# A residual-add RMSNorm whose second tile deals one of its rows unevenly to the DMA engines

## The chip, the cores and the metric

The kernel runs on one core of one Trainium2 chip. The metric is the device time of one execution in microseconds. Times of many executions are given as a median, and one execution was profiled.

## The reference

```python
def reference(x, residual, gamma, eps):     # x, residual: 32 x 2048 x 2048 float32
    z = x + residual
    rms = np.sqrt(np.mean(z ** 2, axis=-1, keepdims=True) + eps)
    return (z / rms * gamma).astype(np.float32)
```

Flattened, there are 65,536 rows of 2048 numbers (8 KB a row). Each row of x and of the residual is read once and each row of the output written once: 1610.6 MB in all.

## The kernel before

**Tiles.** The rows are cut into 74 tiles. A tile of k rows puts k consecutive rows of the input on each of the 128 partitions. The first two tiles (`lead`, line 42) have 3 and 5 rows a partition, the other 72 have `R` = 7. x is loaded into one of two buffers `z[0]`, `z[1]` (even and odd tiles), where everything is computed in place, and the output is stored from there. The residual is loaded into `r_area`, which has room for 11 rows. Even tiles use it from row 4, odd ones from row 0, so that two residuals overlap in the middle; `parts` (line 108 on) splits each tile in two such that the overlapping rows are added first.

**Engines.** Four programs run side by side and meet only at semaphores.

- SyncE issues every DMA (`sync_program`, line 249, and `sp_turn`, line 145). At the start: x and r of tile 0, four small loads of gamma, r and x of tile 1. Then, in the turn of tile i: wait until tile i-1 is scaled, store it (L149); wait until the first part of tile i is added, load r of tile i+1 (L140); wait until the store of tile i-1 has landed, load x of tile i+1 (L134). This order is written out by hand for all tiles; it is no loop on the engine.
- VectorE (`dve_turn`) adds r to x in two parts (L170), then for each part takes the reciprocal of the root (L195) and scales each row by it and by gamma (L175).
- ScalarE (`act_turn`, `act_part`) squares each row and sums it up (L221), then takes the root (L229).
- GpSimd only waits for a last signal (`fin`) from SyncE and clears the semaphores (L328 to L331).

The last tile is handled in four pieces (`tail`), so that its stores begin early.

**Loops.** VectorE and ScalarE run the first `LO` = 3 tiles written out, then a hardware loop over two tiles at a time up to tile `HI` (70 is the last in the loop), then tiles 71 and 72 written out, then the last tile, 73.

**Gamma.** It is loaded to four partitions of `stage`, which is a part of `r_area` that VectorE has set to zero (L274), and spread over all partitions by a shuffle (L276).

[...]

Of the kernel before, what the change touches and what calls it, by code (L numbers as in the profile page):

```python
# [9 lines left out]
def kernel(  # L10
# [14 lines left out]

    nc = tc.nc
    P = nc.NUM_PARTITIONS
    fp32 = mybir.dt.float32  # L30
# [3 lines left out]
    x_f = x.flatten_outer_dims()  # L34
    r_f = residual.flatten_outer_dims()
    o_f = out.flatten_outer_dims()

    n_rows, D = x_f.shape
    R = 7
    STEP = 4  # L40
    U = 16
    lead = [3, 5]
    n_full = (n_rows // P - sum(lead)) // R
    sizes = lead + [R] * n_full
    starts = [0]
    for k in sizes:
        starts.append(starts[-1] + P * k)
    assert starts[-1] == n_rows
    n_tiles = len(sizes)
    last = n_tiles - 1  # L50

    LO = 3
    n_iter = (last - 1 - LO) // 2
    HI = LO + 2 * n_iter
    assert n_iter >= 1

    def rows(t, i):
        k = sizes[i]
        return t[starts[i] : starts[i] + P * k, :].rearrange("(p r) m -> p r m", r=k)

    inv_d = 1.0 / float(D)

    def sb(name, shape):
        return ctx.enter_context(nc.sbuf_tensor(name, shape, fp32))
# [6 lines left out]
    def sem(name):  # L71
        sems.append(ctx.enter_context(nc.semaphore(name)))
        return sems[-1]
# [3 lines left out]
    z = [sb(f"z{p}", [P, R, D]) for p in range(2)]  # L77
    r_area = sb("r_area", [P, R + STEP, D])
    eps_tile = sb("eps_tile", [P, 1])
    ssq = [[sb(f"ssq{p}{h}", [P, 4]) for h in range(2)] for p in range(2)]  # L80
    rms = [[sb(f"rms{p}{h}", [P, 4]) for h in range(2)] for p in range(2)]
    rstd = [[sb(f"rstd{p}{h}", [P, 4]) for h in range(2)] for p in range(2)]
    tail_ssq = sb("tail_ssq", [P, R])
    tail_rms = sb("tail_rms", [P, R])
    tail_rstd = sb("tail_rstd", [P, R])
# [5 lines left out]
    ev = {k: [sem(f"{k}{p}") for p in range(2)] for k in names}  # L91
# [2 lines left out]
    dve = sem("dve_own")  # L94
    act = sem("act_own")
    s_tail = sem("s_tail")
    fin = sem("fin")
    tail_ev = {k: sem(f"tail_{k}") for k in ("add", "rms", "done")}


    tail = [(0, 2), (2, 4), (4, 6), (6, 7)]

    def entry(i):
        if i == 0:
            return R + STEP - sizes[0]
        return 0 if i % 2 else STEP

    def parts(i):
        if i == 0:
            return [(0, 2), (2, sizes[0])]  # L110
        k = sizes[i] if i < 2 else R
        return [(STEP, k), (0, STEP)] if i % 2 else [(0, R - STEP), (R - STEP, R)]

    class Turn:

# [12 lines left out]
    def inc(ins, kind, i):  # L128
        return ins.then_inc(ev[kind][i % 2], U)


    def load_x(sp, t, d=0):
        i = t.i + d
        inc(sp.dma_start(out=z[i % 2][:, : sizes[i], :], in_=rows(x_f, i)), "x_in", i)  # L134

    def load_r(sp, t, d=0):
        i = t.i + d
        e = entry(i)
        inc(
            sp.dma_start(out=r_area[:, e : e + sizes[i], :], in_=rows(r_f, i)),  # L140
            "r_in",
            i,
        )

    def sp_turn(sp, t):
        i = t.i
        t.wait(sp, "done", -1)
        inc(
            sp.dma_start(out=rows(o_f, i - 1), in_=z[(i - 1) % 2][:, : sizes[i - 1], :]),  # L149
            "s_out",  # L150
            i - 1,
        )
        if i == last:
            return
        t.wait(sp, "add_a")
        load_r(sp, t, 1)
        t.wait(sp, "s_out", -1)
        if i + 1 == last:
            for k, (a, b) in enumerate(tail):
                sp.dma_start(  # L160
                    out=z[last % 2][:, a:b, :], in_=rows(x_f, last)[:, a:b, :]
                ).then_inc(x_tail[k], U)
        else:
            load_x(sp, t, 1)


    def add(v, i, a, b):
        e = entry(i)
        s = z[i % 2][:, a:b, :]
        return v.tensor_add(out=s, in0=s, in1=r_area[:, e + a : e + b, :])  # L170

    def scale(v, i, a, b, rs, c=0):
        for g in range(a, b):
            s = z[i % 2][:, g, :]
            ins = v.scalar_tensor_tensor(  # L175
                out=s,
                in0=s,
                scalar=rs[:, c + g - a : c + g - a + 1],
                in1=gamma_tile[:, :],
                op0=mult,  # L180
                op1=mult,
            )
        return ins

    def dve_turn(v, t, own):
        i, p = t.i, t.p
        t.wait(v, "x_in")
        t.wait(v, "r_in")
        (a0, b0), (a1, b1) = parts(i)
        inc(add(v, i, a0, b0), "add_a", i)  # L190
        inc(add(v, i, a1, b1), "add_b", i)
        for h, (a, b) in enumerate(parts(i)):
            n = b - a
            t.wait(v, "rms_a" if h == 0 else "rms_b")
            v.reciprocal(out=rstd[p][h][:, :n], in_=rms[p][h][:, :n]).then_inc(dve, U)  # L195
            v.wait_ge(dve, own(i, h))
            ins = scale(v, i, a, b, rstd[p][h])
        inc(ins, "done", i)
# [34 lines left out]
    def act_turn(s, t, chain):  # L233
        i, p = t.i, t.p
        for h, (a, b) in enumerate(parts(i)):
            chain.wait()
            t.wait(s, "add_a" if h == 0 else "add_b")
            inc(
                act_part(s, chain, z[p], a, b, ssq[p][h], rms[p][h][:, : b - a]),
                "rms_a" if h == 0 else "rms_b",  # L240
                i,
            )

    stage = r_area[:, 5:7, :].rearrange("p r m -> p (r m)")
    stage = stage.rearrange("p (a b) -> p a b", a=16)[:, :, : D // 16]

    def sync_program(sp):
        load_x(sp, Turn(0))  # L250
        load_r(sp, Turn(0))

        sp.wait_ge(tail_ev["add"], 1)
        for q in range(4):
            sp.dma_start(  # L255
                out=stage[32 * q : 32 * q + 1],
                in_=gamma.partition_broadcast(1).rearrange("p (a b) -> p a b", a=16),
            ).then_inc(g_in, U)
        load_r(sp, Turn(1))
        load_x(sp, Turn(1))  # L260
        for i in range(1, n_tiles):
            sp_turn(sp, Turn(i))
        for k, (a, b) in enumerate(tail):
            sp.wait_ge(tail_ev["done"], k + 1)
            sp.dma_start(
                out=rows(o_f, last)[:, a:b, :], in_=z[last % 2][:, a:b, :]
            ).then_inc(s_tail, U)
        sp.wait_ge(s_tail, U * len(tail))
        sp.wait_ge(ev["s_out"][(last - 1) % 2], ((last - 1) // 2 + 1) * U)
        sp.sem_inc(fin, 1)  # L270

    def vector_program(v):
        v.memset(eps_tile[:, :], float(eps))  # L273
        v.memset(stage, 0.0).then_inc(tail_ev["add"], 1)  # L274
        v.wait_ge(g_in, 4 * U)
        v.stream_shuffle(gamma_tile[:, :].rearrange("p (a b) -> p a b", a=16), stage, [0] * 32)  # L276
        for i in range(LO):
            dve_turn(v, Turn(i), lambda i, h: (2 * i + h + 1) * U)
        with v.Fori(0, 2 * n_iter, 2) as it:
            for i in range(LO, LO + 2):  # L280
                dve_turn(v, Turn(i, it), lambda i, h: it * (2 * U) + (2 * i + h + 1) * U)
        for i in range(HI, last):
            dve_turn(v, Turn(i), lambda i, h: (2 * i + h + 1) * U)
        base = 2 * last * U
        t = Turn(last)
        t.wait(v, "r_in")

        def tail_scale(k):
            a, b = tail[k]
            v.wait_ge(tail_ev["rms"], k + 1)  # L290
            v.reciprocal(out=tail_rstd[:, a:b], in_=tail_rms[:, a:b]).then_inc(dve, U)  # L291
            v.wait_ge(dve, base + (k + 1) * U)
            scale(v, last, a, b, tail_rstd, a).then_inc(tail_ev["done"], 1)

        for k, (a, b) in enumerate(tail):
            v.wait_ge(x_tail[k], U)
            add(v, last, a, b).then_inc(tail_ev["add"], 1)
            if k:
                tail_scale(k - 1)
        tail_scale(len(tail) - 1)  # L300

    def scalar_program(s):
# [13 lines left out]
        for k, (a, b) in enumerate(tail):  # L316
# [3 lines left out]
                s, chain, z[last % 2], a, b, tail_ssq[:, a:b], tail_rms[:, a:b]  # L320
            ).then_inc(tail_ev["rms"], 1)

    sync_program(nc.sync)
    vector_program(nc.vector)
    scalar_program(nc.scalar)


    nc.gpsimd.wait_ge(fin, 1)  # L328
    ids = [a.num for a in sems]
    assert ids == list(range(ids[0], ids[0] + len(ids)))  # L330
    nc.gpsimd.sem_clear(range(ids[0], ids[-1] + 1))  # L331


# [33 lines left out]
```

## Time and profile before

| | us |
|---|---|
| Median of 10 executions | 3726.25 (3726.1 to 3726.57) |
| The profiled execution, its own time | 3726.18 |
| Its span in the profile | 3724.4 |
| VectorE busy | 2302.4 (62%) |
| ScalarE busy | 1072.4 (29%) |
| GpSimd busy | 0.2 |
| Data queue, share of 16 engines | 99.9% |
| Moved | 1610.69 MB, 432 GB/s over the span |

The page divides the span into 40 equal slices. For each it gives the busy share of an engine in tenths, the mean busy share of the 16 DMA engines in the same way, and the GB/s that they moved. Lines such as L170 are lines of the kernel's file. A DMA's instruction is short (0.3 to 0.6 us for SyncE to issue one); the transfer itself takes until it lands. For the 7-row tiles the median from issue to landing is 27.2 us for r, 33.8 for x and 34.4 for a store. A window gives the same numbers for any stretch of the span; the DMA share there is the mean over 16 engines, so one engine alone gives 0.06.

### The profile page before, as it was taken

Reading aid. Unit: us, or ns where it says so; the run is one execution under the profiler, and the core shown is the slowest. Engines: PE = TensorE matmul, PEld = TensorE weight load, DVE = VectorE, ACT = ScalarE, POOL = GpSimd, SP = SyncE. Lnnn points to the kernel's source line nnn. Section 1 sums busy time; section 2 is a strip of 40 time slices with the busy share of each in tenths; the row PEclk is TensorE's granted clock in tenths of the full one; section 3 lists DMA queues with packets and bytes.
Section 4 is the critical chain, followed back from the end, with each engine's and each line's share of the span. In section 5 each row is a group of like instructions: output and inputs, shape, how many; then the busy total and the mean of one; then the engine's idle time right before and its main releaser. Section 6 shows DMA issues by size and latency. Waiting matters only on the chain.

```text
span 3724.4 us, 3652 instructions
## 1 busy us (share of the span) xinstructions
DVE 2302.4 (62%) x816; ACT 1072.4 (29%) x1176; POOL 0.2 (0%) x4
## 2 busy tenths in 40 slices
DVE  5666665566665566665566665566665566655566
ACT  2233322233322233322233322233322233322233
POOL 0000000000000000000000000000000000000000
DMA  9999999999999999999999999999999999999999
GB/s 421 431 434 434 435 434 434 434 434 435 434 434 434 434 434 434 434 434 434 434 433 434 434 434 434 434 434 434 434 434 434 434 434 434 434 434 434 433 435 398
DMA packets 32964, 1610.69 MB, mean 432 GB/s; under 512 B 3712, under 2 KB 3776, under 8 KB 3776
## 3 DMA queue, kind: packets, MB, share of 16 engines
q1 hardware_dynamic: 32960, 1610.66, 99.9%
q14 instruction: 4, 0.03, 0.0%
HBM read 1073.77 MB, written 536.87 MB: 432 GB/s over the span
## 4 chain that ended last, share of the span: by engine, by line
DMA 66%; DVE 22%; issue 9%; ACT 2%; SPq 0%; DVEq 0%; ACTq 0%
DMA out_dram<-z 33%; DMA z<-in_x_dram 33%; DVE z L170 15%; DVE z L175 7%; ACT sq_junk L221 1%; DMA r_area<-in_gamma_dram 0%; ACT rms L229 0%; DVE rstd L195 0%; DVEq L126 0%; SPq L255 0%; DVE r_area L274 0%; ACTq L209 0%; ACTq L126 0%; DVE tail_rstd L291 0%; SPq L160 0%
## 5 line engine op out<-in xcount | busy, mean ns | idle before, releaser
L170 DVE TENSOR_TENSOR z<-z,r_area 128x8192 f32<-128x8192 f32 (+2 forms) x150 | 1109.4, 7436 | 1253.3 <-DMA z<-in_x_dram 1227.5
L221 ACT ACTIVATE sq_junk<-z 128x2048 f32<-128x2048 f32 x512 | 963.4, 1882 | 2617.8 <-DVE z L170 2606.4
L175 DVE SCALAR_TENSOR_TENSOR z<-z,rstd,gamma_tile 128x2048 f32<-128x2048 f32 x505 | 1153.5, 2343 | 5.2
L195 DVE RECIPROCAL rstd<-rms 128x4 f32<-128x4 f32 (+2 forms) x146 | 25.2, 173 | 130.9 <-ACT rms L229 130.9
L221 ACT ACTIVATION_READ_ACCUMULATOR sq_junk<-z 128x1 f32 x512 | 95.4, 186 | 0.0
L229 ACT ACTIVATE rms<-ssq,eps_tile 128x4 f32<-128x4 f32 (+2 forms) x146 | 43.3, 297 | 13.4
L175 DVE SCALAR_TENSOR_TENSOR z<-z,tail_rstd,gamma_tile 128x2048 f32<-128x2048 f32 x7 | 16.2, 2345 | 0.1
L276 DVE LOAD_MASK_SELECT gamma_tile<-r_area x1 | 0.0, 14 | 16.1 <-DMA r_area<-in_gamma_dram 16.1
L276 DVE STREAM_SHUFFLE gamma_tile<-r_area 128x2048 f32<-128x2048 f32 x1 | 2.3, 2290 | 0.0
L274 DVE MEMSET r_area<- 128x2048 f32 x1 | 1.8, 1765 | 0.4 <-issue 0.4
L221 ACT ACT_TABLE_LOAD x1 | 1.3, 1283 | 0.9 <-SPq L75 0.9
L229 ACT ACT_TABLE_LOAD x1 | 1.3, 1283 | 0.1
L229 ACT ACTIVATE tail_rms<-tail_ssq,eps_tile 128x2 f32<-128x2 f32 (+1 forms) x4 | 1.2, 295 | 0.1
L273 DVE MEMSET eps_tile<- 128x1 f32 x1 | 0.1, 59 | 1.0 <-SPq L75 1.0
L291 DVE RECIPROCAL tail_rstd<-tail_rms 128x2 f32<-128x2 f32 (+1 forms) x4 | 0.6, 158 | 0.0
L348 POOL MEMSET const-bfloat16-1.0<- 128x1 bf16 x1 | 0.1, 102 | 0.0
L348 POOL MEMSET const-uint8-127<- 128x1 uint8 x1 | 0.1, 101 | 0.0
L348 POOL MEMSET const-float32-0.0<- 128x1 f32 x1 | 0.1, 99 | 0.2 <-issue 0.2
L348 POOL MEMSET const-float32-1.0<- 128x1 f32 x1 | 0.1, 98 | 0.0
## 6 DMA issues: line engine op xcount, KB each, us to landing
r_area<-in_residual_dram SPq DMA_DIRECT2D x72, 7168.0 KB, 27.2
z<-in_x_dram SPq DMA_DIRECT2D x71, 7168.0 KB, 33.8
out_dram<-z SPq DMA_DIRECT2D x71, 7168.0 KB, 34.4
z<-in_x_dram SPq DMA_DIRECT2D x3, 2048.0 KB, 26.3
out_dram<-z SPq DMA_DIRECT2D x3, 2048.0 KB, 14.0
r_area<-in_residual_dram SPq DMA_DIRECT2D x1, 5120.0 KB, 25.1
z<-in_x_dram SPq DMA_DIRECT2D x1, 5120.0 KB, 36.8
out_dram<-z SPq DMA_DIRECT2D x1, 5120.0 KB, 24.7
```

What stands on the lines that cost most here:

```text
L170: return v.tensor_add(out=s, in0=s, in1=r_area[:, e + a : e + b, :])
L175: ins = v.scalar_tensor_tensor(out=s, in0=s, scalar=rs[:, c + g - a : c + g - a + 1], in1=gamma_tile[:, :], op0=mult, op1=mult,)
L195: v.reciprocal(out=rstd[p][h][:, :n], in_=rms[p][h][:, :n]).then_inc(dve, U)
L221: s.activation(out=sq_junk[:, :], in_=src[:, g, :], func=Act.Square, accum_out=sq[:, g - a : g - a + 1],)
L229: return s.activation(out=rm, in_=sq[:, : b - a], func=Act.Sqrt, bias=eps_tile[:, :], scale=inv_d)
L273: v.memset(eps_tile[:, :], float(eps))
L274: v.memset(stage, 0.0).then_inc(tail_ev["add"], 1)
L276: v.stream_shuffle(gamma_tile[:, :].rearrange("p (a b) -> p a b", a=16), stage, [0] * 32)
L291: v.reciprocal(out=tail_rstd[:, a:b], in_=tail_rms[:, a:b]).then_inc(dve, U)
L348: nc = _bacc.Bacc("TRN2", target_bir_lowering=False, num_devices=1)
```

## The change

Four things are edited.

1. **Rows.** The second tile has 4 rows on every partition. Its fifth row, 128 rows of the input in all, is placed in six *patches*. A patch `(e, n, j, r)` puts r rows on each of n partitions, 8e+j, 8(e+1)+j and so on, in the tile's rows 4 to 6. Three patches are moved by DMAs of SyncE, three by DMAs of GpSimd. GpSimd's program adds small loads of a few numbers into a scratch tensor (`tiny`) between its patches, of n partitions each. Each patch moves three times: r, x and the output.
2. **Tile 1.** Rows 4 to 6 of `r_area` (by VectorE) and of `z[1]` (by GpSimd) are set to zero first; SyncE waits for each of the two before it issues the patches' loads, which come before the loads of tile 1. Tile 1 is then computed as a 7-row tile: VectorE waits for the patches, adds rows 4 to 6, waits for x and r, adds rows 0 to 3. SyncE stores its patches behind the store of tile 1, and before the load of x of tile 3 waits for the stores of all patches.
3. **Loops.** `n_iter` is `(last - LO) // 2`, so that the loops of VectorE and ScalarE also take tiles 71 and 72, and nothing is written out between the loop and the last tile.
4. **End.** SyncE no longer waits for the last stores; GpSimd waits for them and clears the semaphores. Ahead of these waits it resets its DMAs (`dma_reset`).

Gamma's `stage` moves to `z[0]`. The diff, cut to its core:

```diff
-    lead = [3, 5]
-    n_full = (n_rows // P - sum(lead)) // R
+    lead = [3, 4]
+    n_full = (n_rows // P - sum(lead) - 1) // R
...
+    sp_patches = [(0, 16, 0, 3), (0, 4, 1, 3), (0, 3, 2, 3)]
+    pool_patches = [(5, 2, 2, 1), (8, 8, 2, 3), (5, 11, 1, 3)]
...
-    n_iter = (last - 1 - LO) // 2
+    n_iter = (last - LO) // 2
...
+    def patch_rows(t, q):
+        n = first_row[q]
+        return t[n : n + q[1] * q[3], :].rearrange("(p r) m -> p r m", r=q[3])
+
+    def patch(area, q):
+        e, n, j, r = q
+        p = 8 * e + j
+        return area[p : p + 8 * (n - 1) + 1 : 8, STEP : STEP + r, :]
...
-        k = sizes[i] if i < 2 else R
-        return [(STEP, k), (0, STEP)] if i % 2 else [(0, R - STEP), (R - STEP, R)]
+        return [(STEP, R), (0, STEP)] if i % 2 else [(0, R - STEP), (R - STEP, R)]
...
+        if i == 2:
+            for q in sp_patches:
+                sp.dma_start(out=patch_rows(o_f, q), in_=patch(z[1], q)).then_inc(m_out, U)
...
         t.wait(sp, "s_out", -1)
+        if i == 2:
+            sp.wait_ge(m_out, len(sp_patches) * U)
+            for k in q_out:
+                sp.wait_ge(k, U)
...
-        t.wait(v, "x_in")
-        t.wait(v, "r_in")
+        if i == 1:
+            v.wait_ge(m_in, 2 * len(sp_patches) * U)
+            for k in q_in:
+                v.wait_ge(k, U)
+        else:
+            t.wait(v, "x_in")
+            t.wait(v, "r_in")
         (a0, b0), (a1, b1) = parts(i)
         inc(add(v, i, a0, b0), "add_a", i)
+        if i == 1:
+            t.wait(v, "x_in")
+            t.wait(v, "r_in")
         inc(add(v, i, a1, b1), "add_b", i)
...
-    stage = r_area[:, 5:7, :].rearrange("p r m -> p (r m)")
+    stage = z[0][:, 3:5, :].rearrange("p r m -> p (r m)")
...
+        for k, t, area in ((0, r_f, r_area), (1, x_f, z[1])):
+            sp.wait_ge(clean[k], 1)
+            for q in sp_patches:
+                sp.dma_start(out=patch(area, q), in_=patch_rows(t, q)).then_inc(m_in, U)
         load_r(sp, Turn(1))
         load_x(sp, Turn(1))
...
-        sp.wait_ge(s_tail, U * len(tail))
-        sp.wait_ge(ev["s_out"][(last - 1) % 2], ((last - 1) // 2 + 1) * U)
-        sp.sem_inc(fin, 1)
...
+        v.memset(r_area[:, STEP:R, :], 0.0).then_inc(clean[0], 1)
...
+    def pool_program(g):
+        g.memset(z[1][:, STEP:R, :], 0.0).then_inc(clean[1], 1)
+        turn = 0
+        g.wait_ge(clean[0], 1)
+        g.wait_ge(clean[1], 1)
+
+        def patches(move):
+            nonlocal turn
+            at = 0
+            for m, q in enumerate(pool_patches):
+
+                n = (q[0] - at) % 16
+                if n:
+                    c = slice(4 * turn, 4 * turn + (4 if n > 1 else 1))
+                    g.dma_start(out=tiny[:n, c], in_=x_f[:n, c]).then_inc(t_in[turn], U)
+                    turn += 1
+                move(m, q)
+                at = (q[0] + q[1]) % 16
+            assert at == 0
+
+        for k, t, area in ((0, r_f, r_area), (n_q, x_f, z[1])):
+            patches(
+                lambda m, q: g.dma_start(
+                    out=patch(area, q), in_=patch_rows(t, q)
+                ).then_inc(q_in[k + m], U)
+            )
+        Turn(1).wait(g, "done")
+        patches(
+            lambda m, q: g.dma_start(
+                out=patch_rows(o_f, q), in_=patch(z[1], q)
+            ).then_inc(q_out[m], U)
+        )
+        for k in q_in + q_out + t_in[:turn]:
+            g.wait_ge(k, U)
...
-    nc.gpsimd.wait_ge(fin, 1)
...
+    nc.gpsimd.dma_reset(range(ids[0], ids[-1] + 1))
+    nc.gpsimd.wait_ge(ev["s_out"][(last - 1) % 2], ((last - 1) // 2 + 1) * U)
+    nc.gpsimd.wait_ge(s_tail, U * len(tail))
     nc.gpsimd.sem_clear(range(ids[0], ids[-1] + 1))
```

More of the change, by code (lines that the diff above doesn't have):

```diff
@@ L41 @@
     U = 16
-    lead = [3, 5]
-    n_full = (n_rows // P - sum(lead)) // R
+    lead = [3, 4]
+    n_full = (n_rows // P - sum(lead) - 1) // R
     sizes = lead + [R] * n_full
     starts = [0]
-    for k in sizes:
-        starts.append(starts[-1] + P * k)
+    for i, k in enumerate(sizes):
+        starts.append(starts[-1] + P * k + (P if i == 1 else 0))
     assert starts[-1] == n_rows
+    sp_patches = [(0, 16, 0, 3), (0, 4, 1, 3), (0, 3, 2, 3)]
+    pool_patches = [(5, 2, 2, 1), (8, 8, 2, 3), (5, 11, 1, 3)]
+    first_row = {}
+    n = starts[1] + P * sizes[1]
+    for q in sp_patches + pool_patches:
+        first_row[q] = n
+        n += q[1] * q[3]
+    assert n == starts[2]
     n_tiles = len(sizes)
@@ L82 @@
     rstd = [[sb(f"rstd{p}{h}", [P, 4]) for h in range(2)] for p in range(2)]
+    tiny = sb("tiny", [16, 64])
     tail_ssq = sb("tail_ssq", [P, R])
@@ L96 @@
     s_tail = sem("s_tail")
-    fin = sem("fin")
+    clean = [sem(f"clean{k}") for k in range(2)]
+    m_in = sem("m_in")
+    m_out = sem("m_out")
+    n_q = len(pool_patches)
+    q_in = [sem(f"q_in{k}") for k in range(2 * n_q)]
+    q_out = [sem(f"q_out{k}") for k in range(n_q)]
+    t_in = [sem(f"t_in{k}") for k in range(3 * n_q)]
     tail_ev = {k: sem(f"tail_{k}") for k in ("add", "rms", "done")}
@@ L321, in scalar_program @@
             ).then_inc(tail_ev["rms"], 1)
+    def pool_program(g):
[29 more added lines that the diff above has]
+            g.wait_ge(k, U)
     sync_program(nc.sync)
+    pool_program(nc.gpsimd)
     vector_program(nc.vector)
     scalar_program(nc.scalar)
-    nc.gpsimd.wait_ge(fin, 1)
     ids = [a.num for a in sems]
     assert ids == list(range(ids[0], ids[0] + len(ids)))
+    nc.gpsimd.dma_reset(range(ids[0], ids[-1] + 1))
+    nc.gpsimd.wait_ge(ev["s_out"][(last - 1) % 2], ((last - 1) // 2 + 1) * U)
+    nc.gpsimd.wait_ge(s_tail, U * len(tail))
     nc.gpsimd.sem_clear(range(ids[0], ids[-1] + 1))
```

## The prediction

> **What bounds the kernel now.** I read the page first, then SyncE's own waits, then the last microseconds cut into windows of 1 us, then the first 20 us as a timeline.
>
> The page, engine shares and slices:
>
> ```profile
> span 3724.4 us, 3652 instructions
> ...
> DVE 2302.4 (62%) x816; ACT 1072.4 (29%) x1176; POOL 0.2 (0%) x4
> ...
> DMA  9999999999999999999999999999999999999999
> GB/s 421 431 434 434 435 434 434 434 434 435 434 434 434 434 434 434 434 434 434 434 433 434 434 434 434 434 434 434 434 434 434 434 434 434 434 434 434 433 435 398
> ```
>
> No engine is full, but the transfers are, in every slice. Only the first slice (421) and the last (398) fall visibly below 434 GB/s. A slice is 93.1 us, so the last one lacks 36/434 x 93.1 = 7.7 us and the first 13/434 x 93.1 = 2.8 us. No other slice has much to give.
>
> SyncE's waits, in the order engine, line, waited for, total, times, longest:
>
> ```profile
> SPq L140 <- DVE z L170: 1689.3, 72, 24.6
> SPq L149 <- DVE z L175: 1191.5, 73, 32.3
> SPq L134 <- DMA out_dram<-z: 696.8, 71, 10.0
> ```
>
> The third is the back-pressure of the transfers: x of the next tile is issued when the store of the tile before has landed, and at that moment a whole r (issued 10 us earlier, worth 7.34 MB / 434 GB/s = 16.9 us) still lies in the queue. So no DMA engine runs dry between tiles, and each of the 16 goes through its own share at its own pace. The end is the end of the slowest one.
>
> The windows at the end show it (columns: stretch, its length, three engines, clock, DMA share of 16 engines, GB/s):
>
> ```profile
> 3715.00:3716.00 1.00, 0.00 (x0) 0.00 (x0) 0.00 (x0) 1.00 1.00 426
> 3716.00:3717.00 1.00, 0.00 (x0) 0.00 (x0) 0.00 (x0) 1.00 0.66 279
> 3717.00:3718.00 1.00, 0.00 (x0) 0.00 (x0) 0.00 (x0) 1.00 0.33 139
> 3718.00:3719.00 1.00, 0.00 (x0) 0.00 (x0) 0.00 (x0) 1.00 0.19 82
> 3719.00:3720.00 1.00, 0.00 (x0) 0.00 (x0) 0.00 (x0) 1.00 0.19 82
> 3720.00:3721.00 1.00, 0.00 (x0) 0.00 (x0) 0.00 (x0) 1.00 0.10 41
> 3721.00:3722.00 1.00, 0.00 (x0) 0.00 (x0) 0.00 (x0) 1.00 0.06 25
> 3722.00:3723.00 1.00, 0.00 (x0) 0.00 (x0) 0.00 (x0) 1.00 0.04 16
> ```
>
> 0.19 x 16 is three engines, 0.06 x 16 is one. Eleven or so finish between 3716 and 3718, three are left from 3718 to 3720, one alone from 3720.6 to 3722.6. The bytes moved after 3716 are 664 KB, 1.5 us for all 16. Evenly dealt, the last byte would move at 3717.5, 5.1 us earlier: that is the whole gain to be had at this end.
>
> [...] In the trace the gamma DMAs of SyncE take 0.59 us each to issue, and GpSimd issues none.
>
> **The change part by part.** One row of 128 partitions is dealt by hand. Adding the patches: engines 0 to 2 get 3+3+3 = 9 rows, 3 gets 6, 4 gets 3, 5 and 6 get 3+1+3 = 7, 7 gets 6, 8 to 15 get 9, together 128. Before, each had 8.
>
> *Price of a row.* 434/16 = 27.1 GB/s per engine, 8192 B is 0.302 us, and a row moves three times (r, x, out): 0.907 us. The deal takes 4.53 us from one engine, 1.81 from two, 0.91 from two, and gives 0.91 to eleven.
>
> *At the end.* The profile doesn't name engines, so I take it that the late ones are those that get fewer rows. The shapes agree: one far behind, two next, two less so. The last ends 3722.6 - 4.5 = 3718.1. The next two (3720.6 and about 3720) end 3718.8 and 3718.2. The fourth and fifth, about 3718, end near 3717.2. The eleven end by 3717 + 0.9 = 3717.9. New last: 3718.8, a gain of **3.8 us**.
>
> *GpSimd waits itself.* SyncE's last wait ends at 3723.27 and GpSimd's clear begins at 3723.32: one hop of 0.05 us goes. The new reset of its DMAs stands before the wait, over 3.5 ms early, so 0.
>
> *Loops to the last but one tile.* Tiles 71 and 72 become one more pass of the loop: VectorE and ScalarE run the same instructions, at 62% and 29%, behind the transfers. 0, and also without that cover it would be a branch in a turn of 50.8 us. Fewer instructions are fetched by the loops, more by SyncE (some 15). All fetches are now
>
> ```profile
> q14 instruction: 4, 0.03, 0.0%
> ```
>
> so one more or less is 8 KB, 0.3 us on one engine.
>
> *The start.* The timeline of before:
>
> ```profile
> 0.96 0.38 SPq L134 DMA_DIRECT2D z<-in_x_dram  x1
> 1.40 0.42 SPq L140 DMA_DIRECT2D r_area<-in_residual_dram  x1
> 1.47 1.76 DVE L274 MEMSET r_area<- 128x2048 f32 x1 [0.40 <-issue]
> 3.26 2.51 SPq L255 DMA_DIRECT2D r_area<-in_gamma_dram  x4
> 5.81 0.58 SPq L140 DMA_DIRECT2D r_area<-in_residual_dram  x1
> 6.43 0.45 SPq L134 DMA_DIRECT2D z<-in_x_dram  x1
> ```
>
> ```profile
> r_area<-in_residual_dram SPq DMA_DIRECT2D x1, 3072.0 KB, 17.2
> out_dram<-z SPq DMA_DIRECT2D x1, 3072.0 KB, 11.4
> ```
>
> Six patch DMAs of SyncE and two waits now stand before r and x of tile 1. VectorE's new memset (3 rows, 3 x 1.76 = 5.3 us) ends at 3.2 + 5.3 = 8.5. GpSimd's memset of 6144 elements isn't in the trace. From below: VectorE's rate, 5.3 us. [...] Then three issues of 0.6 and r at 15.5, x at 16.1 instead of 5.8 and 6.4. Queued behind these waits are the loads of tile 1 alone. The cover is tile 0's own load: r lands at 1.40 + 17.2 = 18.6, so the queue isn't empty before, with 2.5 us to spare. Cost 0, at the worst 1 us.
>
> GpSimd issues 12 DMAs (3 patches and 3 fillers for r, the same for x) before VectorE may add tile 1's patch rows. [...] VectorE is busy with tile 0 until 39.1 anyway. So the 3-row add runs 39.2 to 45.8 (3 x 2.2), and r of tile 2 is issued at 45.8, where before it was 45.64. The full add follows to 54.6 and the last scale ends some 0.4 us later than 72.27. The two extra rows of tile 1 (about 9 us of VectorE) fill what was waiting time. If that cover is gone, see the second rival. The stores of tile 1's patches, three by SyncE (1.8 us) and six DMAs by GpSimd, are needed before x of tile 3. The r of tile 3 issued before it covers about 15 us. Cost 0. I charge **0.2 us** for the start.
>
> Sum: 3726.18 (this execution: span 3724.4 and 1.8 around it; the median of the ten is 3726.25) - 3.8 - 0.05 + 0.2 = **3722.5**.
>
> **Rivals.**
> 1. *Lag comes back.* The 16 arrivals of each load in the trace are 1.2 us apart at 115 us, 3.8 at 524, 4.4 at 2047, 6.5 at the end, and several engines fall behind early and then stay level. If their lag is a distance they settle at and not a share of their bytes, a head start is eaten up: the second, 4 us behind the first, ends at 3720.6 + 0.9 = 3721.5, and the gain is 1.1: **3725.1**. Against it: the last one keeps losing to the end.
> 2. *Patches late* (the slower side). If a GpSimd DMA costs c, the patches land at 11 + 12c + 2, r of tile 2 can move 7.6 us later, and the queue is empty at 39.16 + 11.4 = 50.6. All engines idle for 12c - 30 us: it starts to cost at c = 2.5, undoes the gain at 2.8, and is over 0.2% from 3.4. With c = 4: 18 us, **3740.4**. For it: no GpSimd DMA is in the trace, and the fillers double their number. [...]
> 3. *The deal misses its engines* (the change doesn't do what it says). If GpSimd's shares begin at engine 0 each time, engine 0 has 3+3+3+1+3+3 = 16 rows, 7.3 us more: an early engine then ends at 3717 + 7.3 = 3724.3 instead of 3722.6: **3727.9**. If it's itself a late one, up to 3733.
>
> **Chances.** Forecast 0.58, lag comes back 0.20, deal misses 0.10, late patches 0.12, of which 0.09 is past the bound. A change of 0.2%, 7.5 us, is about what counts as told from none. The end holds only 5.1, so faster is 0.01. Slower is 0.09 and 0.01 from the misses, 0.10. Same is 0.89. The range runs from 3721.0 (the whole 5.1 us) to 3729, past the first and third rival, leaving out the far ends of the second and third.
>
> **What would show it.** Right: three engines no longer alone after 3717, the windows falling from full to nothing within 3 us; r of tile 2 issued near 46 us; DMA slices unchanged. Wrong: a hole in the DMA share at 18 or at 50 us (start), or a tail as long as before with other engines in it (rivals 1 and 3).

## The result and the profile after

| | us |
|---|---|
| Before, median of 28 executions | 3726.35 |
| Changed, median of 8 executions | 3745.92 (3743.73 to 3747.88) |
| Ratio, 95% interval | 1.0053 (1.0044 to 1.0061) |
| Changed, span of the profiled execution | 3745.7 (before 3724.4) |

The change makes the kernel 19.6 us slower, 0.53%. The forecast was 3722.5, with a range up to 3729.

The page of the changed kernel, the lines that answer to those of before:

```profile
span 3745.7 us, 3730 instructions
...
DVE 2316.4 (62%) x819; ACT 1076.4 (29%) x1180; POOL 14.9 (0%) x23
...
DMA  9999999999999999999999999999999999999999
GB/s 362 410 421 429 434 434 432 436 434 432 434 435 433 434 435 434 433 433 435 434 432 434 435 433 433 435 434 432 433 435 434 432 434 435 433 432 436 434 432 397
...
q0 software_dynamic: 576, 1.45, 0.2%
```

The DMA digits are all nines, as before, yet the first four slices have fallen (362, 410, 421, 429, before 421, 431, 434, 434). From slice 5 on nothing has changed, the last slice included. A queue of GpSimd (`software_dynamic`) has appeared with 1.45 MB. So the loss lies in the first tenth of the span (four slices of 93.6 us), and the gain at the end didn't come.

Windows of the changed kernel over the whole of it, with the same columns as in the prediction:

```profile
10.00:50.00 40.00, 19.36 (x10) 7.77 (x9) 6.33 (x12) 1.00 1.02 289
50.00:150.00 100.00, 59.46 (x22) 29.23 (x32) 3.14 (x6) 1.00 0.99 417
150.00:400.00 250.00, 157.06 (x55) 73.07 (x80) 0.00 (x0) 1.00 1.00 426
400.00:3700.00 3300.00, 2043.22 (x716) 949.84 (x1040) 0.00 (x0) 1.00 1.00 434
```

The same windows before:

```profile
10.00:50.00 40.00, 22.68 (x11) 10.07 (x12) 0.00 (x0) 1.00 1.03 441
50.00:150.00 100.00, 66.11 (x24) 32.73 (x35) 0.00 (x0) 1.00 0.99 429
150.00:400.00 250.00, 151.46 (x53) 69.55 (x78) 0.00 (x0) 1.00 1.00 434
400.00:3700.00 3300.00, 2050.93 (x723) 956.49 (x1048) 0.00 (x0) 1.00 1.00 434
```

Divided by 434 GB/s, what is missing is (441-289) x 40 = 14.0 us, then 12 x 100 = 2.8, then 8 x 250 = 4.6, then nothing: 21.4 us, and the spans differ by 21.3. The reader should look at the last two columns of the first line together: the engines count as busy (1.02) and move a third less. They aren't waiting for work. Each transfer takes longer. Finer windows of the changed kernel show how much:

```profile
10.00:20.00 10.00, 0.00 (x0) 0.00 (x0) 6.33 (x12) 1.00 1.13 360
20.00:30.00 10.00, 3.14 (x3) 0.00 (x0) 0.00 (x0) 1.00 0.96 165
30.00:40.00 10.00, 6.33 (x4) 6.37 (x7) 0.00 (x0) 1.00 1.01 252
```

Before, the middle one of these is

```profile
20.00:30.00 10.00, 8.16 (x3) 3.97 (x4) 0.00 (x0) 1.00 1.02 438
```

The trace's records of single packets (384 of 24 KB in the loads and the store of the 3-row tile of before, so one for each of its 128 partitions) say the same: a packet of three rows (24 KB) takes 0.91 us before, and 3.2 to 3.5 us here between 17.5 and 22.5 us (medians of GpSimd's and SyncE's; single ones 1.9 to 4.2).

The start, as a timeline of the changed kernel:

```profile
0.95 5.22 POOL L368 MEMSET z<- 128x6144 f32 x1 [0.51 <-PEq L443]
...
4.47 5.18 DVE L318 MEMSET r_area<- 128x6144 f32 x1 [1.23 <-issue]
9.68 2.07 SPq L304 DMA_DIRECT2D r_area<-in_residual_dram  x3
9.96 0.64 POOL L381 DMA_DIRECT2D tiny<-in_x_dram  x1 [3.79 <-DVE r_area L318]
10.58 0.52 POOL L389 DMA_DIRECT2D r_area<-in_residual_dram  x1
...
13.78 0.42 SPq L167 DMA_DIRECT2D r_area<-in_residual_dram  x1
14.25 0.44 SPq L161 DMA_DIRECT2D z<-in_x_dram  x1
...
26.86 2.29 DVE L320 STREAM_SHUFFLE gamma_tile<-z 128x2048 f32<-128x2048 f32 x1
...
53.13 0.33 SPq L167 DMA_DIRECT2D r_area<-in_residual_dram  x1
```

All the issuing is as early as the prediction had it, or earlier: r of tile 1 at 13.8, GpSimd's DMAs at 0.52 to 0.64 us each, done by 16.3. But gamma, which had landed by 19.35 before,

```profile
19.35 2.29 DVE L276 STREAM_SHUFFLE gamma_tile<-r_area 128x2048 f32<-128x2048 f32 x1
```

now lets VectorE start at 26.86, and r of tile 2 is issued 7.5 us later than the 45.64 of before. GpSimd's last patch of x (11 partitions), issued at 15.81, takes 30.2 us to land:

```profile
z<-in_x_dram POOLq DMA_DIRECT2D x1, 264.0 KB, 30.2
```

That is at 46.0; the prediction had VectorE add the patch rows from 39.2 on.

The end of the changed kernel:

```profile
3737.00:3738.00 1.00, 0.00 (x0) 0.00 (x0) 0.00 (x0) 1.00 0.74 311
3738.00:3739.00 1.00, 0.00 (x0) 0.00 (x0) 0.00 (x0) 1.00 0.39 164
3739.00:3740.00 1.00, 0.00 (x0) 0.00 (x0) 0.00 (x0) 1.00 0.29 123
3740.00:3741.00 1.00, 0.00 (x0) 0.00 (x0) 0.00 (x0) 1.00 0.17 74
3741.00:3742.00 1.00, 0.00 (x0) 0.00 (x0) 0.00 (x0) 1.00 0.14 57
3742.00:3743.00 1.00, 0.00 (x0) 0.00 (x0) 0.00 (x0) 1.00 0.08 33
3743.00:3744.00 1.00, 0.00 (x0) 0.00 (x0) 0.00 (x0) 1.00 0.06 25
```

It is no shorter: from the first dip to the last byte some 7 us, with one engine alone in the last two.

### The profile page after: what moved, and what is told of

It is laid out like the page before. It is cut to its first block, busy times and chain, and to the rows that moved or that the text cites. A ratio compares the mean times of both kernels' runs of the same rounds, so it can differ in the third digit from the quotient of the medians.

```text
span 3745.7 us, 3730 instructions
## 1 busy us (share of the span) xinstructions
DVE 2316.4 (62%) x819; ACT 1076.4 (29%) x1180; POOL 14.9 (0%) x23
## 3 DMA queue, kind: packets, MB, share of 16 engines
q0 software_dynamic: 576, 1.45, 0.2%
## 4 chain that ended last, share of the span: by engine, by line
DMA 67%; DVE 22%; issue 9%; ACT 1%; SPq 0%; DVEq 0%; ACTq 0%
DMA out_dram<-z 33%; DMA z<-in_x_dram 33%; DVE z L204 15%; DVE z L209 7%; ACT sq_junk L263 1%; DMA z<-in_gamma_dram 1%; ACT rms L271 0%; DVE rstd L237 0%; DVEq L153 0%; SPq L297 0%; DVE z L317 0%; SPq L182 0%; ACTq L251 0%; ACTq L153 0%; DVE tail_rstd L335 0%
```

## The experiments

Three theories of the loss stood at first. (A) GpSimd's transfers slow the engines when they run beside SyncE's. (B) The patches' geometry: on which partitions a patch lies. (C) A tile of 4 rows, 32 KB apart in memory, is slow. The trace of before shows nothing of (B), since its tiles lie on all 128 partitions.

The "partition groups" of the expectations are the author's assumption: sets of partitions on which engines that write at once slow each other. The runs show times by layout; how partitions group, or that they do, no run shows. A fourth theory came from the runs: (D) the deal misses its engines, the third rival of the prediction.

| Run | us | over before |
|---|---|---|
| Changed kernel | 3745.92 | +19.6 |
| e1: loops and end alone | 3726.36 | +0.1 |
| e2: the row in one DMA of SyncE | 3727.06 | +0.8 |
| e3: even patches, SyncE, eight apart | 3733.59 | +7.3 |
| e4: the row in one DMA of GpSimd | 3729.21 | +2.9 |
| e5: even patches, eight apart, two by GpSimd | 3737.1 | +10.8 |
| e6: the uneven deal, four apart | 3746.37 | +20.1 |
| e7: even patches, SyncE, adjacent | 3741.77 | +15.5 |
| e8: even deal, four apart, half by GpSimd | 3742.68 | +16.4 |
| e9: e8, GpSimd's round moved by 8 | 3742.57 | +16.3 |
| e10: e6, moved by 8 | 3746.17 | +19.9 |
| e11: changed kernel, moved by 8 | 3745.11 | +18.8 |
| e12: the deal that was really made, SyncE alone | 3745.05 | +18.8 |
| e13: one row fewer on twelve engines | 3730.32 | +3.9 |
| e14: e2 again, beside e13 | 3727.71 | +1.3 |

"Over before" is against the kernel before on the same chip (3726.27 to 3726.41). From e2 on, each is the changed kernel with other patches.

### Parts alone: e1 to e4

e1, the kernel before with

```diff
-    n_iter = (last - 1 - LO) // 2
+    n_iter = (last - LO) // 2
...
+    nc.gpsimd.wait_ge(ev["s_out"][(last - 1) % 2], ((last - 1) // 2 + 1) * U)
+    nc.gpsimd.wait_ge(s_tail, U * len(tail))
```

and SyncE's last waits taken out:

> The kernel before, with only the longer loops and GpSimd's own wait at the end. All theories of the lost 20 us (GpSimd's transfers slow the engines; the geometry of the patches does; the 4-row tile 1 does) put the cause elsewhere: 3726.3, within 0.3 us of before. If instead the loops or the end cost it, 3735 or more.

Measured 3726.36 (ratio 1.0000, 0.9992 to 1.0009). Loops and end cost and bring nothing that can be seen.

e2, with one full-width patch:

```diff
-    sp_patches = [(0, 16, 0, 3), (0, 4, 1, 3), (0, 3, 2, 3)]
-    pool_patches = [(5, 2, 2, 1), (8, 8, 2, 3), (5, 11, 1, 3)]
+    sp_patches = [(0, 128, 0, 1)]
+    pool_patches = []
```

> The changed kernel, but the fifth row of tile 1 is one DMA of SyncE over all 128 partitions (one row each) in place of the six patches; no DMA of GpSimd. If a 4-row tile 1 (32 KB between partitions) is what slows the loads, as slow as the changed kernel: 3740 to 3748. If GpSimd's transfers or the patches' geometry do it: 3725 to 3729.

Measured 3727.06 (1.0002, 0.9994 to 1.0011). (C) falls: the 4-row tile, the two zeroed areas, the 7-row sums of tile 1 and the waits before its loads together cost 0.8 us here and 1.3 in the repeat, e14. The changed kernel's windows against this run's show it at once; e2:

```profile
20.00:30.00 10.00, 8.34 (x3) 3.79 (x3) 0.00 (x0) 1.00 1.07 455
```

e3, with `sp_patches = [(0, 16, 0, 3), (0, 16, 1, 3), (0, 16, 2, 2)]` and none of GpSimd:

> The changed kernel, but the row is dealt evenly in three patches of 16 partitions, eight apart, 3+3+2 rows, all by SyncE; no DMA of GpSimd and no filler. If patches on partitions eight apart are slow by their geometry: 3733 or more, with packets of 24 KB over 1.5 us. If GpSimd's transfers are the cause: 3725 to 3729, packets of 0.91 us.

Measured 3733.59 (1.0020, 1.0012 to 1.0028). Its windows:

```profile
20.00:30.00 10.00, 8.81 (x4) 3.13 (x3) 0.00 (x0) 1.00 0.96 241
30.00:40.00 10.00, 7.22 (x6) 4.63 (x7) 0.00 (x0) 1.00 0.98 419
```

The 24 KB packets took 1.9 us, twice 0.91, with the engines busy (a DMA share of 0.96) and no GpSimd transfer in the program. This is what (B) forecasts, and (A) isn't needed for it. Why it is twice, no run shows.

e4, with `pool_patches = [(0, 128, 0, 1)]` and none of SyncE:

> The changed kernel, but the row is one DMA of GpSimd over all 128 partitions; no patches, no fillers. If any GpSimd transfer beside SyncE's slows the engines: 3733 or more, and 20 to 40 us into the span under 300 GB/s. If it takes the patches' geometry or the uneven deal: 3725 to 3729.

Measured 3729.21 (1.0008, 0.9999 to 1.0017), just above the second range. Between 20 and 30 us it has

```profile
20.00:30.00 10.00, 7.54 (x4) 0.90 (x1) 0.00 (x0) 1.00 1.07 453
```

and packets of 0.31 us for one row: GpSimd's transfers don't slow the others as such here. It is 2.1 us above e2, and each of its 12 executions is slower than each of e2's 12. For a row over all partitions (A) is no more than that.

### The geometry, and a deal that misses: e5 to e8

e5, `sp_patches = [(0, 16, 0, 3)]`, `pool_patches = [(0, 16, 1, 3), (0, 16, 2, 2)]`:

> The even deal on partitions eight apart (three patches of 16, 3+3+2 rows), two of the three issued by GpSimd, no fillers. Geometry and GpSimd's cost (7.3 and 2.1 us as measured alone) simply add: 3735 to 3737. If two queues that write the same partition groups at once slow each other further: 3739 or more, with packets of 24 KB over 2.5 us.

Measured 3737.1 (1.0029, 1.0018 to 1.0039): between the two, near the plain sum of 7.3 and 2.1. The 24 KB packets took 1.9 us in the middle, at most 2.5, between 14 and 35 us.

e7, e3 with `p = 16 * j` and a step of 1, so that a patch lies on 16 adjacent partitions:

> The even deal by SyncE alone, but each patch of 16 on 16 adjacent partitions[...]. Theory of partition groups: packets of 24 KB at 3.6 us (four times 0.91; eight apart it was 1.9, twice), and 3740 to 3748. If the 1.9 us came from many engines reading rows close together in HBM: the same 1.9 us and 3733 as with partitions eight apart.

Measured 3741.77 (1.0042, 1.0025 to 1.0059). Its windows:

```profile
20.00:30.00 10.00, 8.18 (x4) 1.53 (x1) 0.00 (x0) 1.00 1.02 127
30.00:40.00 10.00, 6.22 (x6) 6.24 (x9) 0.00 (x0) 1.00 0.92 277
```

The 24 KB packets took 3.0 to 3.6 us: 0.91 us before on all 128 partitions, 1.9 in e3 on partitions eight apart, 3.0 to 3.6 here on adjacent ones. The time goes with the layout on the partitions here, and rows close together in memory aren't the cause, since they were as close together in e3 as here. The 3.6 was forecast from the assumption of groups; that it came near doesn't show what the groups are.

e6 and e8 put each patch on partitions four apart in one half of the 128 (`p = 64 * (e // 8) + 4 * (e % 8) + j`, step 4). e6 keeps the uneven deal, e8 deals evenly, engines 0 to 7 by SyncE and 8 to 15 by GpSimd behind fillers of 8. Engine numbers are those of the deal here and below, since the trace names no engine: 0 is the one with which SyncE's patches are taken to begin. That a filler moves GpSimd's next patch on by its own number of engines, in a round of 16, is an assumption of the author's; no trace of before shows it.

> The changed kernel with its own deal (9,9,9,6,3,7,7,6, then 9 on engines 8 to 15), but each patch put on partitions four apart, in one half of the partitions[...]. Theory of partition groups: packets of 24 KB near 0.91 us again, the loss at the start falls to 2 to 5 us, and if the uneven deal shortens the end as predicted, 3724 to 3728. If GpSimd's patches and fillers were the cause: still 3738 or more. If the lag at the end comes back: 3728 to 3732, with a last engine 4 us behind the next.

> As the run on own partition groups, but dealt evenly, 8 rows to each engine: three patches of SyncE on engines 0 to 7, three of GpSimd on 8 to 15 with a filler of 8 before each. Its difference to the uneven one is what the uneven deal alone brings: by the prediction 3.8 us (this one 3728 to 3731), by the rival of the lag that comes back 1 or less.

Measured 3746.37 (1.0052, 1.0036 to 1.0069) and 3742.68 (1.0046, 1.0029 to 1.0062). The expectation of e8 failed, and e6 fell where GpSimd's patches or fillers are the cause: an even deal on partitions four apart was 16.4 us slow. Every DMA of before has 16 arrivals in its trace (3712 for 232 DMAs). What had gone wrong stands in the 16 of r of tile 1 in the trace of e8, us after the first:

```
e8:   0.0  0.2  0.4  0.8  1.0  1.0  1.2  1.8 | 9.5  9.6  9.6  9.7 10.0 10.1 10.2 10.4
```

Eight have come within 1.8 us, and eight are 9.5 to 10.4 us late. If GpSimd's patches went to engines 0 to 7 too, these had 16 rows and the others none, and r and x of 16 rows are 2 x 16 x 0.302 = 9.7 us. The 24 KB packets were slow as well (1.5 to 1.8 us); why isn't shown.

### GpSimd's round, moved by 8: e9 to e11

If GpSimd's round merely stood 8 off, moving everything on by 8 would mend it:

```diff
-                n = (q[0] - at) % 16
+                n = (q[0] + 8 - at) % 16
...
-                at = (q[0] + q[1]) % 16
+                at = (q[0] + 8 + q[1]) % 16
```

with a filler behind the last patch that closes the round.

> The even deal on own partition groups, but GpSimd's DMAs are moved on by eight in their round: a patch where the filler of 8 stood and a filler where the patch stood. In the even run before, r of tile 1 landed on eight engines 9.5 us later than on the other eight, as if GpSimd's patches had gone to engines 0 to 7, which SyncE's patches load already. If GpSimd's round stands 8 off: the patches now go to 8 to 15, each engine has 8 rows, the spread falls under 3 us, 3726 to 3730. If GpSimd's DMAs begin at engine 0 each time, whatever came before: nothing changes, 3741 to 3744.

> The uneven deal on own partition groups, moved on by eight in GpSimd's round in the same way. If the round stands 8 off, this is the deal that was meant[...]: 3722 to 3727, and a shorter tail. If GpSimd's DMAs begin at engine 0 each time: as the run without the move, 3744 to 3748.

> The changed kernel as it is, on partitions eight apart, with GpSimd's fillers set so that its patches move on by eight in the round. If the round stands 8 off: the deal is the meant one, what is left is the price of partitions eight apart and of GpSimd's patches, 7 to 11 us: 3730 to 3738. If GpSimd's DMAs begin at engine 0 each time: as the changed kernel, 3743 to 3748.

Measured 3742.57, 3746.17 and 3745.11: each as its counterpart without the move (3742.68, 3746.37 and 3745.92), 0.1 to 0.8 us below it. The fillers don't move anything that these times show. In e9, half of SyncE's 24 KB patch packets between 24 and 32 us (16 of 32) took 0.92 to 1.05 us, so a patch of eight partitions isn't slow by itself. In e10 the arrivals have four steps:

```
e10:  0.0  0.0  0.2  0.2  0.5  0.5  0.5  0.8 | 7.7  7.7  7.8  8.0 | 11.6 | 16.5 16.7 16.7
```

If every GpSimd DMA begins at engine 0, engines 8 to 15 have no row, 4 to 7 have 12 (2 x 12 x 0.302 = 7.2 us), engine 3 has 15 (9.1) and 0 to 2 have 21 or 22 (13.3): eight, four, one, three, as measured, though the later steps are larger than the sum (11.6 us for 9.1, and 16.5 to 16.7 for 13.3). Packets took longer as well: at a DMA share of 1.02 the engines moved 311 GB/s between 30 and 40 us.

### The deal that was made, without GpSimd: e12

If every GpSimd DMA begins at engine 0, the changed kernel dealt 16, 16, 15 and 12 rows to engines 0 to 3, 9 to each of 4 to 7, 6 to 8 to 10, and 3 to 11 to 15. SyncE can make that deal:

```diff
+    sp_patches = [(0, 16, 0, 3), (0, 11, 1, 3), (0, 8, 2, 3), (0, 4, 3, 3), (0, 3, 4, 3), (0, 2, 5, 1)]
+    pool_patches = []
```

> The deal that the changed kernel has if GpSimd's DMAs always begin at engine 0 (16, 16, 15 and 12 rows on engines 0 to 3, 9 on 4 to 7, 6 on 8 to 10, 3 on 11 to 15), made by SyncE alone with six patches of 16, 11, 8, 4, 3 and 2 partitions that begin at engine 0; each engine's rows lie in its own eight partitions. If the loss is the deal (8 rows too many on engine 0, 7.3 us)[...], and not GpSimd: 3738 to 3746. If the deal costs nothing by itself: 3733 to 3736, as the even deal by SyncE. If GpSimd's own transfers are most of it: under 3733.

The range of 3738 to 3746 has e3's 7.3 us in it beside the 7.3 of the deal. Measured 3745.05 (1.0050, 1.0033 to 1.0066), 0.9 us below the changed kernel. Its arrivals of r of tile 1 come in steps of five, three, four, one and three (last ones 0.4, 2.0, 4.1, 5.9 and 7.9 us), which is what 16, 11, 8, 4 and 3 or 2 partitions give if each patch of SyncE puts one partition on each engine from the same first one on. Beside them those of the changed kernel itself, cut in the same places:

```
e12:      0.0  0.0  0.2  0.3  0.4 | 1.7  1.8  2.0 | 3.5  3.8  3.9  4.1 | 5.9 | 7.5  7.6  7.9
changed:  0.0  0.2  0.6  0.7  1.3 | 1.9  2.0  2.1 | 2.3  2.5  3.3  3.5 | 3.9 | 6.1  6.7  7.4
```

The steps are less sharp, but three are far behind the rest (6.1 to 7.4 us). The deal that was meant has nine rows on eleven engines and fewer on five, so eleven would be last together, at most 2 x 6 x 0.302 = 3.6 us after the first. The windows of e12:

```profile
10.00:50.00 40.00, 22.48 (x10) 11.15 (x12) 0.00 (x0) 1.00 1.01 339
50.00:150.00 100.00, 56.36 (x21) 25.85 (x30) 0.00 (x0) 1.00 0.98 416
150.00:400.00 250.00, 157.06 (x55) 73.07 (x80) 0.00 (x0) 1.00 0.99 422
```

Against 441, 429 and 434 of before these are 9.4, 3.0 and 6.9 us, 19.3 in all. (D) and (B) together make a loss of the whole size without GpSimd's queue. Stage by stage the two runs differ: up to 50 us e12 loses 9.4 us where the changed kernel loses 14.0, and its 24 KB packets take 1.9 us between 17.5 and 22.5 us where those took 3.2 to 3.5, so the second queue, or patches on other partitions than those of e12, makes the first stage slower; after 50 us e12 loses more. From 150 to 400 us, where no patch moves any more, both still lose (4.6 and 6.9 us). Part of it is engines without work (in e12 the DMA share is 0.91 from 150 to 175 us, before it is 1.01), part is single slow packets of the full loads and stores: in the changed kernel 17 of 176 between 175 and 200 us take over 2.3 us, up to 3.6, for the usual 2.12 (before: 1 of 191). Why stays open. No run has (D) without (B).

### The end by itself: e13 and e14

No run so far took a row off the late engines without the loss at the start. e13 tries, with one patch on 112 partitions (meant as 7 rows for each engine) and two meant for engines 0 to 3:

```diff
+    sp_patches = [(0, 112, 0, 1), (0, 4, 0, 2), (0, 4, 1, 2)]
+    pool_patches = []
```

> The row by SyncE alone: one DMA of 112 partitions (7 rows on each engine) and 16 rows on engines 0 to 3 in two patches of four partitions four apart, so that engines 0 to 3 have 11 rows and the other twelve 7, one fewer than in the run with one DMA of 128 partitions. If a row less at the start is 0.907 us less at the end, as the prediction took it, 0.9 us below that run (about 3726.2), the last engine being one of 4 to 7. If the lag comes back whatever was dealt, no gain: 3727 or, with what the small patches cost, 3728.

> The run with one DMA of 128 partitions for the row, once more on the same chip, for the comparison: 3727.1 again, within 0.3.

Measured 3730.32 and 3727.71. Both lie outside what was expected: e14 is 0.6 us above e2, and its executions spread from 3726.6 to 3729.9. e13 is 2.6 us slower than e14, so there is no gain to be seen, but it doesn't settle the question: its single-row packets took 0.50 to 0.60 us where e14's took 0.31, and how its rows lay on the engines isn't shown. Its windows and those of e14:

```profile
20.00:30.00 10.00, 8.81 (x4) 3.30 (x3) 0.00 (x0) 1.00 1.04 296
```

```profile
20.00:30.00 10.00, 8.16 (x3) 3.98 (x4) 0.00 (x0) 1.00 1.05 449
```

That alone is (449-296)/434 x 10 = 3.5 us, more than the difference of the medians.

## Why the prediction was wrong

**What bounds the kernel** was read rightly. The spans follow what the DMA engines move (changed kernel: 21.4 us missing, 21.3 longer; e12: 19.3 and 19.4), and the added computing on VectorE, ScalarE and GpSimd shows as no more than 0.1 us in e1 and 0.8 in e2.

**The sixteen shares.** The step that failed first is the one under the deal, that a GpSimd DMA goes on in a round where the one before left off, so that a filler can place the next patch. It was the author's assumption: in the trace of before GpSimd issues no DMA. In e6 and e8 to e11 the arrivals and times fit GpSimd patches, all of 11 partitions or fewer, that begin at engine 0 each time, as SyncE's do, whatever went before, and e12, which makes the deal that follows for the changed kernel, has its time within 0.9 us. The number for the third rival's deal, 16 rows on engine 0, fits too, and it was given a chance of 0.10. A step on which a change stands and which no trace shows deserved a larger chance of failing. It is not the only failure: the even deal of e3, without any DMA of GpSimd, still costs 7.3 us.

**Price of that miss.** 8 rows too many are 7.3 us, as the rival had it, but the rival let them fall on engines that end early anyway and arrived at 3727.9. The loss came at the start, and it was not one engine's: up to 50 us the changed kernel lost 14.0 us of what all 16 engines move, with packets in hand (a DMA share of 1.02). Where a lag grew larger, engines also ran dry behind the waits that join the first tiles, so the early ones could not simply run on to "the end of the slowest one"; e10 shows it:

```profile
50.00:60.00 10.00, 2.27 (x1) 0.00 (x0) 0.00 (x0) 1.00 0.69 294
```

**"I charge 0.2 us for the start."** This term is the mis-sized one: the start cost 14.0 us up to 50 us, and 21.4 with what followed. The working counted when DMAs are issued and when the queue would be empty, and there it held: r of tile 1 at 13.8 (the 15.5 of the working rested on a longer memset of GpSimd, which no trace of before shows), GpSimd's memset 5.22 us (5.3 at VectorE's rate), its DMAs 0.52 to 0.64 us each, and the issue margin sufficed, the DMA share being 0.96 or more from 10 to 60 us. When they land it had wrong: 46.0, where VectorE was to add the patch rows from 39.2 on. It took for granted that a row on an engine costs 0.302 us wherever it lies. In e3, on partitions eight apart, a 24 KB packet takes 1.9 us for 0.91; in the changed kernel, with GpSimd's patches beside them, 3.2 to 3.5. e3 prices the first alone at 7.3 us, the miss is 7.3 by the sum, and e12 has 18.8. The 4.2 between are not separated. Extra rows that move at half or a third of the pace would make the two multiply rather than add, but that is argued and not shown.

**Rival 2, late patches,** came close in time, 3740.4, for another reason. It needed GpSimd DMAs of 4 us and a hole in the DMA share at 50 us. No trace of before shows the 4 us, the start at 11 or the 2 us for landing that it reckons with. GpSimd took 0.52 to 0.64 us for each, and the changed kernel has no hole (1.00 from 50 to 60 us). That the time came near is chance.

**The end.** The gain of 3.8 us didn't come: the deal that was to bring it was not made, so the step itself is neither shown nor refuted. Two things can be read from e10, if each engine is followed by its lag from transfer to transfer. The engine that is last at the end is one of the four of the second step, 4 to 7 by the deal: it goes from 3.8 us behind at 942 us to 7.7 at the end, which agrees with the assumption that late engines were given fewer rows. And what becomes of a lag depends on when it is made. The 16.7 us at r of tile 1 are 0.9 at 83 us, after the hole. The stores of the patches then make a new one, with three engines 6.0 to 7.1 us behind at 128 us, and it stays: 6.0 to 6.9 at 2008 us. So there an offset that was made after the last hole was not eaten up, which speaks against rival 1 as a general rule. Whether a lead of 4.5 us of the late engine would have lasted to the end was tried in e13 and stays open.

**Loops and GpSimd's wait:** 0, as forecast (e1; the forecast 0.05 is below what can be told).

## What to carry to other kernels

A DMA share of 1.0 says that engines have packets in hand, not that they move 27 GB/s each (165 GB/s for all 16 at a share of 0.96): read the GB/s beside it. A fall of it at full share meant here that packets took longer, and then one packet's time is the thing to look at. Patches of 16 partitions were priced here by where they lay, not by their bytes: the same 128 rows, all by SyncE, cost 7.3 us on partitions eight apart (e3) and 15.5 on adjacent ones (e7), and as one row over all 128 partitions 0.8 and 1.3 (e2, e14). And a deal by engine has to be seen in the arrivals of one transfer before any gain is reckoned on it.

## What the runs showed of the hardware that was not expected

- DMAs of GpSimd on 8 and on 3 partitions went to the same engines as SyncE's, by all signs from the same first one on: in e8 eight arrivals of r of tile 1 are 9.5 to 10.4 us behind, in e10 the steps are of eight, four, one and three. Small DMAs ahead of them did not move them on (e9 to e11 are 0.1 to 0.8 us below the same deals without the move). For the 11 partitions of the changed kernel, the time of e12, 0.9 us below, and the arrivals beside it say so.
- 24 KB packets: 0.91 us on all 128 partitions (before), 1.9 on partitions eight apart (e3), 3.0 to 3.6 on 16 adjacent ones (e7); on partitions four apart in one half 1.5 to 1.8 (e8), and 0.92 to 1.05 for 16 of 32 of SyncE's (e9).
- In one DMA over 112 partitions a packet of one row (8 KB) takes 0.50 to 0.60 us, in one over 128 partitions 0.31 (e13, e14).
- Moving one row of 128 partitions by GpSimd instead of SyncE cost 2.1 us (e4 against e2).
- Clearing 128 x 6144 float32 numbers took GpSimd 5.22 us and VectorE 5.18 (changed kernel).
